# Twelve unit pairs a layer by seven quarter products, with their weight sums built in scratch memory by copies and accumulating transfers

## The chip, the core and the metric

The kernel runs on one core of one Trainium2 chip. The metric is the device time of one execution in microseconds; the median of the runs shown counts. The core has a matrix engine (PE in the profile, with its weight loads as PEld), a vector engine (DVE), a scalar engine (ACT), GpSimd (POOL) and SyncE (SP), which issues nearly all DMA transfers. Each engine works through its own list of instructions in order and waits at semaphores for the others.

## The reference

Two layers over 512 tokens of width 1024, all in float32. A layer has a mixing part (a gated DeltaNet of 8 heads, a windowed attention of 16 heads with a window of 128, a gated merge and an output projection) and a feed-forward part of width 4096:

```python
h2 = rmsnorm(x, pre_mlp_g)
ff = jnp.square(jax.nn.relu(h2 @ w_ff1)) @ w_ff2
return x + rmsnorm(ff, post_mlp_g)
```

The change concerns `h2 @ w_ff1`, a product of 512 x 1024 by 1024 x 4096, and what has to be ready for it.

## The kernel before

**Precision.** Every large product is made of three matmuls: each operand is split into a rounded high part and a rest, and high x high, high x rest and rest x high are added up in PSUM. A weight chunk (128 x 1024 elements, 512 KB) is loaded from the packed weights into a buffer `wr` (L282, six buffers), ACT makes the high part `wh` (L384), DVE the rest `wl` (L385), four buffers each. `prefetch` keeps four chunks ahead of their use.

**The stages of a layer.** First the input projections `ps_b`; then a mixing stage of 16 rounds (the loop `for i in range(16)`). Each round has one or two projections of the DeltaNet keys (`k_unit`) or the merge gates, and one of 16 attention groups (`att_group`: block `t` of 128 tokens, key head `g`, half `e`). For `t > 0` POOL masks the probabilities of the own block into `pc` (L1017) and PE uses them in `ps_o` (L1023). POOL also makes the rotary products (`rt`, L911 to L916) and the powers `irk` (L829). A head stage follows (8 DeltaNet heads, with small stores `fd` on POOL's queue), then the up projections and the output projection, and then the feed-forward part.

**The feed-forward part** runs over four slabs `s` of 1024 columns of `w_ff1`. Each slab is 8 units of 128 columns. A plain unit is 24 matmuls of 512 columns (8 blocks of rows, three matmuls each). A pair of units can instead be computed by seven products of quarters (a scheme of the Strassen kind): 7 x 4 x 3 = 84 matmuls of 256 columns, in `ff1`. For this the pair needs, beside its raw weights, the sums of quarters x0 to x3 (the two halves of the first unit and of the second): x0+x2, x0+x2+x3, x2+x3 and x0+x1+x2+x3, in two chunks `a` and `b`. Before, DVE makes them in SBUF from the two loaded chunks (L343, four additions of 128 x 512 a pair). `SEQ` says which units are paired: none in slab 0, two pairs in slab 1, three in slab 2 and four in slab 3, nine a layer. After slabs 0 to 2 the product with `w_ff2` follows, again by seven products (`mm_c`, P1 to P7), whose last half may be held back (`pending`) into the first pair of the next slab.

**What sets the order.** The kernel is written as one straight list of instructions over both layers. A scheduler then places them engine by engine by their dependences and its own model of times. An instruction that depends on nothing may be placed far ahead of where it is written; only blocks of the class `Order` (such as all matmuls in `ff1`) hold their written order. Transfers of SP's queue use eight completion counters in turn, those of POOL's queue eight others; a transfer waits for the one eight before it on its queue.

Of the kernel before, what the change touches and what calls it, by code (L numbers as in the profile page):

```python
# [15 lines left out]
ALU = mybir.AluOpType  # L16
# [25 lines left out]
WR = 6  # L42
FF_ORDER = (0, 4, 1, 5, 2, 6, 3, 7)
XB = 6
SEQ = (FF_ORDER, (0, 1, (4, 5), (2, 3), 6, 7), ((0, 1), (4, 5), (2, 3), 6, 7), ((0, 1), (2, 3), (4, 5), (6, 7)))

MIX = "G K K G K K G K K G K K G GA GA GA".split()
NA = sum(c.count("A") for c in MIX)
# [79 lines left out]
def hybrid_trunk(ctx, tc, x, positions, pre_mix_g, dn_conv_w, dn_a_log, dn_dt_bias, dn_norm_g,  # L128
# [44 lines left out]
    def PZ(name):  # L173
        return pp.tile([P, 512], F32, name=name, tag="ss", bufs=2)
# [147 lines left out]
    def up_specs(l, s):  # L322


        out = []

        def unit(m):
            return load(("w_ff1", l, 0, (s * 8 + m) * P, 0))

        def one(ms):  # L330
            b = {}

            def raw():
                b["0"], b["1"] = (unit(m) for m in ms)
                return b["0"]

            def of(n_):
                b[n_] = wp.tile([P, 1024], F32, name="wr", bufs=WR)
                x0, x1, x2, x3 = b["0"][:, :512], b["0"][:, 512:], b["1"][:, :512], b["1"][:, 512:]
                yb = b["a"][:, 512:]  # L340
                for o_, i0, i1 in (((b[n_][:, :512], x0, x2), (yb, b[n_][:, :512], x3)) if n_ == "a" else
                                   ((b[n_][:, 512:], x2, x3), (b[n_][:, :512], yb, x1))):
                    tt(out=o_, in0=i0, in1=i1, op=ALU.add)  # L343
                return b[n_]

            return raw, lambda: of("a"), lambda: of("b"), lambda: b["1"][:, 512:]

        last = None
        for n, e in enumerate(SEQ[s]):
            two = isinstance(e, tuple)  # L350
            if two:
                raw, fa, fb, tail = one(e)
            out.append((raw if two else lambda m=e: unit(m), 0))
            if last:
                out.append((last, -1))
            last = None
            if two:
                out += [(fa, 0), (fb, 0)]
                last = tail
        return out + [(last, -1)] * bool(last)  # L360

    specs = []
    for kind_, *key in chunk_order(depth):
# [241 lines left out]
    for l in range(depth):  # L605
# [435 lines left out]


        late, klate = (), []
        for i in range(16):
            us = []
            for c in MIX[i]:
                u = kind[c](n_[c])
                n_[c] += 1
                if u:
                    next(u)  # L1050
                    us.append(u)
            for u in klate:
                fin(u)
            klate = us
            g = att_group(*groups[i])
            next(g)
            fin(late)
            late = g
            if i > LASTK:
                steps(3)  # L1060
# [251 lines left out]
        for h in range(2):  # L1312
            d_keys(h)
            d_decay(h)
            d_turn(h)
        for h in range(H):
            if h < H - 2:
                d_keys(h + 2)
            d_inverse(h)
            d_load(h + 4)  # L1320
            d_chain(h)
            d_step(h - 2, h - 1)
            if h < H - 2:
                d_decay(h + 2)
                d_turn(h + 2)
            if h < H - 1:
                d_dense(h + 1)
# [12 lines left out]
            first.append((ps, mm_a(ps, yT, range(6))))  # L1340
        mT = []
        for m in range(KT):
            if m % 4 == 0:
                mq = UQ("mbr")
                sq = UQ("sgr") if m < NA2 else None
            qs = slice(m % 4 * 512, (m % 4 + 1) * 512)
            mb = mq[:, qs]
            dma(mb, mbd[m])
            if m < NA2:
                sga[m] = sq[:, qs]  # L1350
                dma(sga[m], gad[m])
            if m < 4:
                ps = first[m][0]
                mm_a(ps, yT, range(6, KT), first[m][1])
            else:
                ps = PM("ps_ud")
                mm_a(ps, yT)
            stt(out=sga[m], in0=sga[m], scalar=1.0, in1=ps, op0=ALU.add, op1=ALU.mult)
            tt(out=mb, in0=mb, in1=sga[m], op=ALU.add)
            p_ = pair(T[m % 4], "mT")  # L1360
            act(out=p_[0], in_=mb, func=AF.Copy, scale=0.5)
            stt(out=p_[1], in0=mb, scalar=0.5, in1=p_[0].bitcast(F32), op0=ALU.mult,
                op1=ALU.subtract)
            mT.append(p_)
# [100 lines left out]
        def ff1(done, rest=None):  # L1465


            order = Order(nc.tensor)
            order.begin()
            for n, e in enumerate(SEQ[s]):  # L1470
                if not isinstance(e, tuple):
                    ps = PM("ps_f1")
                    w = weights()
                    if rest is None and not any(isinstance(x, tuple) for x in SEQ[s][n + 1:n + 2]):
                        mm_a(ps, h2, w=w)
                        done((e,), ps)
                        continue
                    mm_a(ps, h2, range(4), w)
                    last = rest

                    def rest(ps=ps, w=w, e=e):
                        mm_a(ps, h2, range(4, 8), w)
                        done((e,), ps)

                    if last:
                        last()
                        rest()
                        rest = None
                    continue

                R = X4("raw")
                a, y, z, q = PM("ps_a"), PZ("ps_y"), PS("ps_z"), PK("ps_q")
                a, y, z, q = (b[:, half(0)] for b in (a, y, z, q))
                q_ = R[:, half(2)]
                c1 = weights()
                mm_h(a, c1, 0, ops["a11"], True)
                nc.scalar.copy(y, a)
                rest()

                def seventh():  # L1500
                    c = weights()
                    mm_h(q, c, 4, ops["n3"], True)
                    nc.scalar.copy(q_, q)
                    return c

                c2 = weights()
                mm_h(y, c2, 4, ops["n2"], False)
                nc.scalar.copy(z, y)
                mm_h(a, c1, 4, ops["a12"], False)
                act(out=R[:, half(0)], in_=a, func=AF.Relu)  # L1510
                if n > 0:
                    c3 = seventh()
                mm_h(z, c2, 0, ops["n1"], False)
                if n == 0:
                    c3 = seventh()
                act(out=R[:, half(3)], in_=z, func=AF.Copy, scale=-1.0)
                tt(out=R[:, half(3)], in0=R[:, half(3)], in1=q_, op=ALU.subtract)

                def rest(e=e, R=R, y=y, z=z, q_=q_, c3=c3):
                    mm_h(y, c3, 0, ops["a22"], False)  # L1520
                    tt(out=R[:, half(2)], in0=y, in1=q_, op=ALU.add)
                    act(out=R[:, 512:], in_=R[:, 512:], func=AF.Relu)
                    mm_h(z, weights(), 0, ops["n4"], False)
                    act(out=R[:, half(1)], in_=z, func=AF.Relu, scale=-1.0)
                    act(out=R, in_=R, func=AF.Square)
                    done(e, R)
            if rest:
                rest()
            order.end()

        cg = combos()
        for s in range(3):
# [9 lines left out]
            def lefts(X, Y):  # L1542

                a11, a21, a12, a22 = X[:, 0:512], X[:, 512:1024], Y[:, 0:512], Y[:, 512:1024]
                make("P1", T[5], a11)
                s1, s2 = T[4]("S1"), T[4]("S2")
                tt(out=s1, in0=a21, in1=a22, op=ALU.subtract)
                make("P5", T[7], s1)
                tt(out=s2, in0=a11, in1=s1, op=ALU.subtract)
                make("P6", T[1], s2)  # L1550
                make("P4", T[2], a22, -1.0)
                tt(out=s1, in0=a21, in1=a11, op=ALU.subtract)
                tt(out=s2, in0=a12, in1=s2, op=ALU.subtract)
                for name, src in (("P2", a12), ("P7", s1), ("P3", s2)):
                    later[name].append(src)
# [7 lines left out]
            def done(ms, ps):  # L1563
                if len(ms) == 2:
                    raw[ms[0] // 4] = ps
                else:
# [4 lines left out]
                    act(out=r_, in_=ps.rearrange("p (a n) -> p a n", a=2), func=AF.Relu)  # L1571
                    act(out=r_, in_=r_, func=AF.Square)
                count[0] += len(ms)
                if count[0] % 4 == 0:
                    lefts(*raw)

            if all(not isinstance(e, tuple) for e in SEQ[s]):
                for i, m in enumerate(SEQ[s]):
# [4 lines left out]
                        mm_a(ps, h2)  # L1583
                    done((m,), ps)
                    if s == 0 and i in (1, 3, 5):
                        next(cg)
            else:
                ff1(done, pending)
            pa = [PZ("ps_pa") for t in range(2)]
            mm_c(pa, left["P1"])  # L1590
            py = [PM("ps_py") for t in range(2)]
            for t in range(2):
                act(out=py[t], in_=pa[t], func=AF.Copy, scale=-1.0)
            make_later("P2", T[5])
# [99 lines left out]
```

## Time and profile before

| What | us |
|---|---|
| median of 3 runs | 1817.67 |
| lowest and highest of them | 1816.85 and 1820.55 |
| the profiled execution, its own time | 1816.19 |
| span of that execution, first to last instruction | 1814.5 |
| PE busy (and share of the span) | 1794.6 (99%) |
| DVE busy | 1375.1 (76%) |
| ACT busy | 1007.5 (56%) |
| POOL busy | 210.6 (12%) |
| DMA engines, share of the span for SP's queue | 49.2% |

Times in the profile count from the first instruction of the span. The mixing stage of layer 0 with its 16 rounds lies between about 45 and 240 us, the head stage up to 480, the feed-forward part of layer 0 from about 590 to 900; the second layer has the same stages some 900 us later. A row of a timeline has start and duration in us, the engine, the line, the operation, the tile written and the tiles read, and in brackets how long the engine had been idle before it and what ended that. A group's row has busy time and mean ns of one, then the idle time before and its releasers. In the list of waits stand the waiting instruction, what it waited for, the us in total, the times and the longest.

### The profile page before, as it was taken

How to read it: one execution, taken by the hardware profiler on the slowest of the kernel's cores; microseconds unless marked ns; L12 is line 12 of the kernel's file. 1: busy time of each engine (PE TensorE's matmuls, PEld its weight loads, DVE VectorE, ACT ScalarE, POOL GpSimd, SP SyncE). 2: the span in 40 equal slices, each digit the busy share in tenths (PEclk: the TensorE clock that was granted, in tenths of full speed). 3: DMA queues.
4: the chain of work that ended last, by engine and by line, in shares of the span. 5: the costliest groups of instructions: out<-in, count | busy, mean ns of one | idle time of the engine just before them, and what ended most of it. 6: DMA issues, size and time to landing. Idle time of an engine off the chain costs nothing.

```text
span 1814.5 us, 28394 instructions
## 1 busy us (share of the span) xinstructions
PE 1794.6 (99%) x10252; PEld 1524.7 (84%) x10252; DVE 1375.1 (76%) x2590; ACT 1007.5 (56%) x2065; POOL 210.6 (12%) x386
## 2 busy tenths in 40 slices
PE   9999999999999999999999999999999999999998
PEld 8878878888788888989898887888877888889896
DVE  5499796887666878898556997968875669698973
ACT  6678742444434656566556877234443347566572
POOL 0322102221101000000013221022111010000000
PEclk9999999999999999999999999999999999999999
DMA  5633447655463254554445334585545533555551
GB/s 201 203 112 121 111 146 226 178 172 152 117 208 129 82 164 156 174 180 145 168 160 176 106 127 111 169 232 159 163 140 154 171 116 105 174 162 164 174 178 56
DMA packets 146431, 278.60 MB, mean 154 GB/s; under 512 B 33569, under 2 KB 66657, under 8 KB 146290
## 3 DMA queue, kind: packets, MB, share of 16 engines
q1 hardware_dynamic: 145778, 276.75, 49.2%
q8 instruction: 81, 1.33, 0.3%
q14 instruction: 60, 0.49, 0.1%
q0 software_dynamic: 512, 0.03, 0.0%
HBM read 239.38 MB, written 37.36 MB: 153 GB/s over the span
## 4 chain that ended last, share of the span: by engine, by line
PE 88%; DVE 4%; ACT 4%; DMA 2%; issue 1%; POOL 0%; SPq 0%; DVEq 0%; POOLq 0%; ACTq 0%
PE ps_b L459 3%; PE ps_b L461 3%; PE ps_b L463 3%; PE ps_f L400 2%; PE ps_f L401 2%; PE ps_f L402 2%; PE ps_us L400 2%; PE ps_ud L400 2%; PE ps_us L401 2%; PE ps_ud L401 2%; PE ps_ud L402 2%; PE ps_us L402 2%; PE ps_vp L400 2%; PE ps_vp L402 2%; PE ps_vp L401 1%; PE ps_qp L401 1%
## 5 line engine op out<-in xcount | busy, mean ns | idle before, releaser
L384 ACT CAST wh<-wr 128x1024 fp32r<-128x1024 f32 (+2 forms) x368 | 372.7, 1019 | 430.4 <-PE ps_us L401 60.2
L385 DVE TENSOR_TENSOR wl<-wr,wh 128x1024 fp32r<-128x1024 f32 (+2 forms) x368 | 434.9, 1189 | 183.8 <-ACT wh L384 180.2
L526 POOL TENSOR_TENSOR pr<-pq,pw 128x1 f32<-128x1 f32 x16 | 9.8, 615 | 790.1 <-DVE pq L525 790.1
L459 PE MATMUL ps_b<-wh,h_h 128*128 128x432 f32 (+1 forms) x192 | 71.1, 370 | 0.0
L461 PE MATMUL ps_b<-wl,h_h 128*128 128x432 f32 (+1 forms) x192 | 70.4, 367 | 0.0
L463 PE MATMUL ps_b<-wh,h_l 128*128 128x432 f32 (+1 forms) x192 | 70.3, 366 | 0.0
L400 PE MATMUL ps_f<-g_h,wh 128*128 128x512 f32 x160 | 62.4, 390 | 0.0
L401 PE MATMUL ps_f<-g_l,wh 128*128 128x512 f32 x160 | 62.4, 390 | 0.0
L402 PE MATMUL ps_f<-g_h,wl 128*128 128x512 f32 x160 | 62.2, 389 | 0.0
L401 PE MATMUL ps_qp<-h_l,wh 128*128 128x512 f32 x128 | 53.9, 421 | 0.0
L400 PE MATMUL ps_vp<-h_h,wh 128*128 128x512 f32 x128 | 53.7, 420 | 0.0
L402 PE MATMUL ps_vp<-h_h,wl 128*128 128x512 f32 x128 | 53.7, 419 | 0.0
L995 ACT ACTIVATE M<-M,nm 128x128 f32<-128x128 f32 x128 | 49.8, 391 | 5.9 <-DVE nm L990 5.8
L400 PE MATMUL ps_qp<-h_h,wh 128*128 128x512 f32 x128 | 51.8, 405 | 0.0
L343 DVE TENSOR_TENSOR wr<-wr 128x512 f32<-128x512 f32 x72 | 47.5, 685 | 5.5 <-DMA wr<-in_weights_dram 5.2
L400 PE MATMUL ps_kp<-h_h,wh 128*128 128x512 f32 x128 | 51.6, 403 | 0.0
L402 PE MATMUL ps_qp<-h_h,wl 128*128 128x512 f32 x128 | 51.4, 401 | 0.0
L401 PE MATMUL ps_vp<-h_l,wh 128*128 128x512 f32 x128 | 51.3, 401 | 0.0
L401 PE MATMUL ps_ga<-h_l,wh 128*128 128x512 f32 x128 | 51.0, 398 | 0.0
L400 PE MATMUL ps_gb<-h_h,wh 128*128 128x512 f32 x128 | 51.0, 398 | 0.0
L402 PE MATMUL ps_kp<-h_h,wl 128*128 128x512 f32 x128 | 50.9, 398 | 0.0
L402 PE MATMUL ps_ga<-h_h,wl 128*128 128x512 f32 x128 | 50.7, 396 | 0.0
(435 smaller groups left out, 5928.4 us busy)
## 6 DMA issues: line engine op xcount, KB each, us to landing
wr<-in_weights_dram SPq DMA_DIRECT2D x320, 512.0 KB, 3.6
wr<-in_weights_dram SPq DMA_DIRECT2D x24, 432.0 KB, 5.2
D<-dd SPq DMA_DIRECT2D x32, 256.0 KB, 2.7
xd<-xo SPq DMA_DIRECT2D x12, 512.0 KB, 3.0
xt<-xd SPq DMA_DIRECT2D x24, 256.0 KB, 4.5
D<-gd SPq DMA_DIRECT2D x16, 256.0 KB, 6.2
dd<-D SPq DMA_DIRECT2D x16, 256.0 KB, 5.2
kkd<-kk SPq DMA_DIRECT2D x16, 256.0 KB, 2.0
```

Of the source, the lines that this page charges most:

```text
L343: tt(out=o_, in0=i0, in1=i1, op=ALU.add)
L384: nc.scalar.copy(wh[:, :w], wr[:, :w])
L385: sub(out=wl[:, :w], in0=wr[:, :w], in1=wh[:, :w].bitcast(F32), op=ALU.subtract)
L400: mm(ps, lhsT=wh[:, k, :], rhs=hi, start=k == 0, stop=False)
L401: mm(ps, lhsT=wh[:, k, :], rhs=lo, start=False, stop=False)
L402: mm(ps, lhsT=wl[:, k, :], rhs=hi, start=False, stop=k == KT - 1)
L459: mm(pss[t], lhsT=hi[:, tsl], rhs=wh[:, r, :], start=k == 0 and not onto, stop=False, skip_group_check=onto)
L461: mm(pss[t], lhsT=hi[:, tsl], rhs=wl[:, r, :], start=False, stop=False, skip_group_check=onto)
L463: mm(pss[t], lhsT=lo[:, tsl], rhs=wh[:, r, :], start=False, stop=k == KT - 1, skip_group_check=onto)
L526: ptt(out=r, in0=q1, in1=mhalf[:, 0:1], op=ALU.pow)
L995: act(out=M[:, j * P:(j + 1) * P], in_=M[:, j * P:(j + 1) * P], func=AF.Exp, bias=nm[:, j:j + 1], accum_out=den[:, j:j + 1])
```

## The change

All units of slabs 1, 2 and 3 are paired: 12 pairs a layer. The two chunks of sums are no longer made on DVE. For each of the 24 pairs there is a scratch tensor of 128 x 2048 in device memory (`fs` and a number: fs_112 to fs_123 are layer 0's pairs, fs_124 to fs_135 layer 1's in the built program), filled in four steps: two copies of the raw weights (L372, 512 KB each, SP's queue); an accumulating transfer from the weights (L374, 512 KB, POOL's queue); and two accumulating transfers inside the scratch tensor (L376 and L378, 256 KB each, POOL's queue). Each step reads what the step before has written. A generator `prepare(l)` issues them; it is advanced at 16 places of the layer: five in the mixing rounds, four among the heads, four among the up projections, three in slab 0. A pair then loads one raw chunk, the two chunks of sums and the second half of its other raw chunk. The halves of the sums have changed places, so the two products that use them swap their half. Beside this, the P1 operands are made as soon as their half of a slab is there, and two pairs of PSUM buffers change places for slabs 1 and 2.

```diff
-SEQ = (FF_ORDER, (0, 1, (4, 5), (2, 3), 6, 7), ((0, 1), (4, 5), (2, 3), 6, 7), ((0, 1), (2, 3), (4, 5), (6, 7)))
+FF_PAIRS = ((0, 1), (4, 5), (2, 3), (6, 7))
+SEQ = (FF_ORDER, FF_PAIRS, FF_PAIRS, ((0, 1), (2, 3), (4, 5), (6, 7)))
...
         def one(ms):
-            b = {}
-
-            def raw():
-                b["0"], b["1"] = (unit(m) for m in ms)
-                return b["0"]
-
-            def of(n_):
-                b[n_] = wp.tile([P, 1024], F32, name="wr", bufs=WR)
-                x0, x1, x2, x3 = b["0"][:, :512], b["0"][:, 512:], b["1"][:, :512], b["1"][:, 512:]
-                yb = b["a"][:, 512:]
-                for o_, i0, i1 in (((b[n_][:, :512], x0, x2), (yb, b[n_][:, :512], x3)) if n_ == "a" else
-                                   ((b[n_][:, 512:], x2, x3), (b[n_][:, :512], yb, x1))):
-                    tt(out=o_, in0=i0, in1=i1, op=ALU.add)
-                return b[n_]
-
-            return raw, lambda: of("a"), lambda: of("b"), lambda: b["1"][:, 512:]
+            d = sums[l, s, ms]
+
+            def of(c, w=1024):
+                wr = wp.tile([P, 1024], F32, name="wr", bufs=WR)
+                dma(wr[:, :w], d[:, c * 1024:c * 1024 + w])
+                return wr
+
+            def tail():
+                wr = wp.tile([P, 1024], F32, name="wr", bufs=WR)
+                dma(wr[:, :512], wpk[index["w_ff1", l, 0, (s * 8 + ms[1]) * P, 0], :, 512:])
+                return wr
+
+            return lambda: unit(ms[0]), lambda: of(0), lambda: of(1), tail
...
+    pairs = [(s_, e) for s_, seq in enumerate(SEQ) for e in seq if isinstance(e, tuple)]
+    sums = {(l, *p): dr.tile([P, 2048], F32, name=f"fs{l}{p[0]}{p[1][0]}")
+            for l in range(depth) for p in pairs}
+
+    def prepare(l):
+        def stages(s_, e):
+            i = index["w_ff1", l, 0, (s_ * 8 + e[0]) * P, 0]
+            assert index["w_ff1", l, 0, (s_ * 8 + e[1]) * P, 0] == i + 1
+            v = sums[l, s_, e][:, :].rearrange("p (h t c) -> p h t c", h=2, t=2)
+            for t in range(2):
+                dma(v[:, :, t, :], wpk[i + t].rearrange("p (h c) -> p h c", h=2))
+            yield
+            pdma(v[:, :, 1, :], wpk[i:i + 2, :, 0:512].rearrange("t p c -> p t c"), accum_op=ALU.add)
+            yield
+            pdma(v[:, 0, 0, :], v[:, 1, 1, :], accum_op=ALU.add)
+            yield
+            pdma(v[:, 1, 0, :], v[:, 0, 0, :], accum_op=ALU.add)
+
+        todo = [stages(*p) for p in pairs]
+        for n in range(len(todo) + 3):
+            for g in todo[max(n - 3, 0):n + 1]:
+                next(g, None)
+            yield
...
+        ready = prepare(l)
         for i in range(16):
+            if i % 3 == 1:
+                next(ready)
...
         for h in range(H):
+            if h % 2:
+                next(ready)
...
         for m in range(KT):
+            if m in (1, 3, 5, 7):
+                next(ready)
...
                 c2 = weights()
-                mm_h(y, c2, 4, ops["n2"], False)
+                mm_h(y, c2, 0, ops["n2"], False)
...
-                mm_h(z, c2, 0, ops["n1"], False)
+                mm_h(z, c2, 4, ops["n1"], False)
...
             def lefts(X, Y):
-                make("P1", T[5], a11)
...
                 count[0] += len(ms)
+                if ms[-1] in (1, 3):
+                    make("P1", T[5], raw[0][:, 0:512])
...
                     if s == 0 and i in (1, 3, 5):
+                        next(ready, None)
                         next(cg)
...
-            pa = [PZ("ps_pa") for t in range(2)]
+            pa = [(PM if s else PZ)("ps_pa") for t in range(2)]
...
-            py = [PM("ps_py") for t in range(2)]
+            py = [(PZ if s else PM)("ps_py") for t in range(2)]
```

Where the scheduler puts the new transfers, at three places of layer 0's mixing stage. (Lines of the changed file stand lower: L283 is the weight load L282, and 24 lines lower stand L802, that was L778, L1041 (L1017), L853 (L829) and L837 (L813).)

SP's list, around the first stores of keys `kkd`. Before:

```order
L282 DMA wr<-in_weights_dram 128x1024 x7
L813 DMA kkd<-kk 128x512
L816 DMA D<-dd 128x512
L282 DMA wr<-in_weights_dram 128x1024
L813 DMA kkd<-kk 128x512
```

Now:

```order
L283 DMA wr<-in_weights_dram 128x1024
L372 DMA fs_118<-in_weights_dram 256x512 x2
L283 DMA wr<-in_weights_dram 128x1024
L372 DMA fs_119<-in_weights_dram 256x512 x2
L372 DMA fs_120<-in_weights_dram 256x512 x2
L283 DMA wr<-in_weights_dram 128x1024
L372 DMA fs_121<-in_weights_dram 256x512 x2
L837 DMA kkd<-kk 128x512
```

Two to four copies stand between one weight load and the next. The copies begin behind the tenth weight load with fs_112 and end with fs_135, layer 1's last pair, all in this stage.

POOL's list a little later, with the counters that each instruction waits for (DMAHW: transfers of SP's queue, DMASW: those of POOL's):

```order
L374 DMA fs_121<-in_weights_dram 256x1x512 [waits DMAHW2_49,DMASW2_49]
L378 DMA fs_120<-fs_120 128x512 [waits DMASW0_49]
L853 TENSOR_TENSOR irk<-ssk,pw 128x4 [waits DVE_49]
L376 DMA fs_121<-fs_121 128x512 [waits DMAHW1_49,DMASW2_49]
L374 DMA fs_122<-in_weights_dram 256x1x512 [waits DMAHW7_49,DMASW5_49]
L378 DMA fs_121<-fs_121 128x512 [waits DMASW4_49]
L376 DMA fs_122<-fs_122 128x512 [waits DMAHW4_49,DMASW5_49]
```

Before, between two `irk` there stands no transfer. Now the three steps of a pair wait for one another on POOL, with one or two steps of a neighbouring pair between them.

POOL's list around the masks `pc` of rounds 8 and 9. Before:

```order
L829 TENSOR_TENSOR irk<-ssk,pw 128x4
L1017 AFFINE_SELECT pc<-pf_h 128x512
L1017 AFFINE_SELECT pc<-pf_l 128x512
L1017 AFFINE_SELECT pc<-pf_h 128x512
L1017 AFFINE_SELECT pc<-pf_l 128x512
```

Now:

```order
L1041 AFFINE_SELECT pc<-pf_h 128x512
L374 DMA fs_135<-in_weights_dram 256x1x512
L1041 AFFINE_SELECT pc<-pf_l 128x512
L378 DMA fs_134<-fs_134 128x512
L1041 AFFINE_SELECT pc<-pf_h 128x512
```

These are the two halves of the fifth mask and the first half of the sixth. The L376 of fs_135 stands behind them, between the two halves of the sixth, its L378 behind the sixth, and then, behind one `irk`, comes the seventh mask. Ahead of the first mask stand 47 of the 72 accumulating transfers, ahead of the seventh all of them.

## The prediction

> **What bounds the kernel now.** I read the page first, then the idle time of TensorE by place, then the DMA load by stretch.
>
> ```profile
> span 1814.5 us, 28394 instructions
> PE 1794.6 (99%) x10252; PEld 1524.7 (84%) x10252; DVE 1375.1 (76%) x2590; ACT 1007.5 (56%) x2065; POOL 210.6 (12%) x386
> PEclk9999999999999999999999999999999999999999
> DMA  5633447655463254554445334585545533555551
> q1 hardware_dynamic: 145778, 276.75, 49.2%
> q0 software_dynamic: 512, 0.03, 0.0%
> ```
>
> TensorE is busy for 99% of the span at full granted clock; no other engine comes near it. So only two things can move the end: fewer or shorter matmuls, or a wait that TensorE does not have now. Whether shorter matmuls pay must be read from starts, since a record of 0.39 us overlaps the next one. The timeline of TensorE, around one plain unit and one pair of the third slab of layer 0:
>
> ```profile
> 664.15 0.39 PE L400 MATMUL ps_f<-g_h,wh 128*128 128x512 f32 x1
> ...
> 672.31 0.28 PE L487 MATMUL ps_a<-g_h,wh 128*128 128x256 f32 x1
> ...
> 676.49 0.28 PE L487 MATMUL ps_y<-n_h,wh 128*128 128x256 f32 x1
> ...
> 692.33 0.40 PE L400 MATMUL ps_f<-g_h,wh 128*128 128x512 f32 x1
> ```
>
> From 664.15 to 672.31 stand 36 matmuls of 512 columns: 8.16 / 36 = 0.2267 us each. From 676.49 to 692.33 stand 132 of 256 columns: 15.84 / 132 = 0.1200 us each. Half the columns cost 53% of the time, not 50%.
>
> The stretches, with all engines' busy time, granted clock, share of the DMA engines and GB/s:
>
> ```profile
> core 0: us, PE busy (x) PEld busy (x) DVE busy (x) ACT busy (x) POOL busy (x), PEclk, DMA share, GB/s
> 17.00:128.00 111.00, 109.08 (x576) 97.07 (x575) 72.96 (x199) 76.81 (x201) 23.11 (x50) 1.00 0.49 162
> 128.00:185.00 57.00, 56.99 (x301) 46.44 (x299) 53.18 (x156) 45.46 (x136) 16.52 (x28) 1.00 0.40 121
> 600.00:900.00 300.00, 300.00 (x1698) 264.35 (x1697) 245.08 (x304) 186.98 (x293) 1.62 (x3) 1.00 0.48 157
> 17.00:22.00 5.00, 5.00 (x31) 4.81 (x30) 3.43 (x12) 2.99 (x9) 0.82 (x2) 1.00 0.96 342
> ```
>
> In the feed-forward stretch (600 to 900) TensorE is busy for all 300 us. The last row is the fastest DMA stretch I found: 342 GB/s at a share of 0.96, so 342 / 0.96 = 356 GB/s is the most that the 16 engines are seen to do.
>
> **The change, part by part.**
>
> *Three more pairs a layer, six in all.* Two plain units are 48 matmuls of 512 columns, 48 x 0.2267 = 10.88 us; a pair is 84 of 256, 84 x 0.1200 = 10.08 us. Gain 0.80 us a pair, 6 x 0.80 = 4.8 us, all of it on the path, since TensorE has no idle time there.
>
> *The sums on VectorE go away.*
>
> ```profile
> L343 DVE TENSOR_TENSOR wr<-wr 128x512 f32<-128x512 f32 x72 | 47.5, 685 | 5.5 <-DMA wr<-in_weights_dram 5.2
> ```
>
> 47.5 us of VectorE leave, and 6 x 1.5 splits of a whole chunk come in. Both lie beside the matmuls of the feed-forward stretch, where VectorE has 55 of 300 us free; worth nothing either way. The swapped halves of the sums, the earlier P1 and the exchanged PSUM buffers are reorderings inside that same full stretch: nothing. If that cover were gone, the 5.2 us of waits in this row are what could return.
>
> *The weights of a pair.* Before, a pair loads 2 x 512 KB; now 3 x 512 + 256 KB, 1.84 MB in 10.08 us, 182 GB/s. That is half of 356, so it hides under the matmuls.
>
> *The building of the sums.* This decides. A pair has two copies of 512 KB from weights to scratch on SP's queue and three accumulating transfers of 512, 256 and 256 KB on POOL's: 2 x 0.524 = 1.05 MB copied and 1.05 MB added. For 24 pairs that is 25.2 MB copied and 25.2 MB added. The text of the kernel spreads them over each layer, but as the rows of the built order show (the section on the change), the scheduler puts the transfers of both layers, all 24 pairs, into the first layer's mixing stage. They begin behind the first weight loads at about 17 us, and the last accumulate stands on POOL ahead of the seventh pair of L1017 (L1041 in the new file), the masked copies of attention scores. In the trace these are:
>
> ```profile
> 127.81 0.64 POOL L1017 TENSOR_SCALAR_AFFINE_SELECT pc<-pf_h 128x512 fp32r<-128x512 f32 x1 [0.76 <-ACT pf_h L500]
> ...
> 185.17 0.63 POOL L1017 TENSOR_SCALAR_AFFINE_SELECT pc<-pf_h 128x512 fp32r<-128x512 f32 x1 [3.22 <-ACT pf_h L500]
> ```
>
> The first of them is at 127.8 us and the seventh at 185.2 us. Their readers are matmuls; by line, and in the list of waits:
>
> ```profile
> L1023 PE MATMUL ps_o<-pc,vp x24: 387/397/504, 131.0 to 236.8; 128*128 128x512 f32 x24
> PE ps_o L1023 <- POOL pc L1017: 0.6, 1, 0.6
> PEld ps_o L1023 <- POOL pc L1017: 4.7, 14, 1.0
> ```
>
> TensorE already waits for them now and then, by up to 1.0 us: there is no reserve. POOL works in order, and each accumulate waits there until the one before it of its pair has landed. So 72 accumulates must be through by 185.2 us; whatever they are late is late for TensorE. Behind the waiting POOL stand the rotary products, the 1/norms and the masks; behind a late weight load on SP stand the splits and every matmul.
>
> The room for them, by the DMA view of 17 to 185 us:
>
> ```profile
> DMA packets 12639, 24.83 MB, mean 148 GB/s; under 512 B 1680, under 2 KB 4816, under 8 KB 12624
> q1 hardware_dynamic: 12624, 24.65, 45.4%
> q8 instruction: 7, 0.11, 0.3%
> q14 instruction: 8, 0.07, 0.1%
> wr<-in_weights_dram SPq DMA_DIRECT2D x23, 512.0 KB, 4.0
> ```
>
> The engines now use 45.8% of the 168 us, 77 us; 91 us are free. No row shows a copy from device memory to device memory, nor an accumulate. Bounds by the nearest rows: at the least each byte costs one pass at the best rate, 25.2 / 0.356 = 71 us for the copies and 71 for the accumulates: 77 + 71 + 71 = 219, 51 us too many. At the most a copy is two passes (it reads and writes the same memory) and an accumulate three (it reads two operands and writes one): 77 + 141 + 212 = 430, 262 too many. I take one pass for a copy, as for a load, and two for an accumulate, because it fetches two operands for each result: 77 + 71 + 141 = 289, 121 us too many.
>
> The Trainium skill, in "Collectives: The Full Stack", The bandwidth ceiling: the fold count and why AG ≠ RS ≠ AR, says that a sum inside a DMA costs not the addition but the second read, which halves the rate; by it the accumulates cost the 141 us that I take, where the row of a load would give 71. Its page "DMA: Bandwidth & Descriptors", Latency and other measured facts, gives 207 to 214 GB/s for copies between HBM tensors; by 214 the copies are 118 us and the sum 168 too many. No run here shows either yet.
>
> *Other costs of the 120 new transfers.* The nearest row for one on POOL's queue is the 2 KB store of the head's scale:
>
> ```profile
> L1216 POOL DMA_DIRECT2D fd<-ff x16: 590/620/757, 348.9 to 1393.3; - x16
> DMA to landing us min/median/max: 1.7/2.4/4.5
> ```
>
> 0.62 us of issue, x72 = 45 us of POOL, beside the 23 + 17 us that it is busy in the two windows: 85 of 168, not the bound. The second layer's mixing stage gets no transfers, so it stays as it is.
>
> **Sum.** The profiled execution has 1816.2 us, 1.7 more than its span; - 4.8 + 121 = 1932.4. It lies 1.5 under the median of 1817.7, so against the median I predict 1934, slower.
>
> **Rivals.**
>
> *All hidden (the other side).* The transfers find gaps, nothing reaches TensorE and only the matmuls count: 1817.7 - 4.8 = 1812.9. For it: the engines are free for 91 of the 168 us, and behind 240 us nothing is added but 0.79 MB a pair. Against it: 50.3 MB in the free 91 us would be 553 GB/s, over the 356 seen. It decides at the first L1041: if POOL has issued its 47 earlier accumulates by 127.8 us, this is right. Partly hidden, with up to 8 us left over, it reads as no change.
>
> *The chain, not the bytes.* The transfers are cheap, and only the order on POOL counts. A step takes the 2.4 us of the small store to land, plus its bytes at 356 GB/s: (2.4 + 1.47), (2.4 + 0.74), (2.4 + 0.74), 10.2 us a pair. With two pairs under way that is 24 x 10.2 / 2 = 122 us, against 168 less the 40 that POOL is busy, 128: not late at all. With 1.25 under way, about what the built order allows near its end (a step waits for the one before, and one step of the next pair fits between), 195 - 128 = 67 us late. For it: each wait on POOL is of this kind. Against it: it needs the DMA engines to have room, which the sum denies. Its middle, 4 to 47 us late, gives 1817 to 1860; below that it is the case before.
>
> *Heavy transfers.* Two passes for a copy and three for an accumulate: 1817.7 - 4.8 + 262 = 2075. For it: every byte is read from and written to the same memory. Against it: loads and stores of this trace go at one pass each.
>
> *It does not do what it says.* The pairs are built once and read later, so the spread in the text would be the truth only if the scheduler kept it; the built order shows that it does not, so this has no chance of its own.
>
> **How the numbers follow.** Forecast, +50 to +210 us, 64%; chain or light transfers, 1817 to 1860, 13%; heavy, over 2030, 12%; all hidden 6%; partly hidden 5%. The predicted time is 1934. The range takes in the light end and most of what lies above: 1826 to 2040. A change of 0.2%, 3.6 us, is about what a measurement can tell from none. Faster by more: 0.06; within: 0.06, the partly hidden and a piece of the light case; slower: 0.88.
>
> **What would show it.** In the profile after: DMA tenths of 8 and 9 in the first 5 to 8 slices, and TensorE's busy tenths under 9 there; `ps_o` waiting for `pc` for tens of us in total, with the POOL row before it released by a DMA; the q0 row with 25 MB or more; the stretch of feed-forward of both layers shorter by 2.4 us each and full. The second layer's mixing stage as long as before, 240 us. I am wrong if the seventh `pc` stands before 200 us, or if the feed-forward stretch, and not the first 250 us, holds the loss.

## The result and the profile after

The changed kernel takes 2000.0 us (median of 4 runs, 1998.6 to 2005.9), the kernel before 1818.0 us: 1.1005 times as long, 95% interval 1.098 to 1.103. I had predicted 1934 us in a range from 1826 to 2040. The direction and the place were right; the loss is 182 us where I had said 116.

The page of the changed kernel, the rows that answer to those quoted of before:

```profile
span 2004.2 us, 29122 instructions
PE 1816.7 (91%) x10468; PEld 1548.6 (77%) x10468; DVE 1347.5 (67%) x2542; ACT 1024.4 (51%) x2101; POOL 275.6 (14%) x458
PE   9475045899999999999999999999999999999998
PEclk9787567899999999999999999999999999999999
DMA  9899789547655553456574543447554543556672
q0 software_dynamic: 13952, 25.20, 8.8%
```

TensorE was busy for 99% of the span and is now for 91%. Nearly all of its gaps lie in the first eight slices of 50 us; the DMA engines are at 7 to 9 tenths in seven of them, and behind them both rows look as before. The accumulating transfers are the 25.2 MB of q0.

Two stretches by engine, with the columns of the prediction's stretches: from the first weight loads to the issue of the last accumulate, and the 112 us behind it.

```profile
17.00:368.00 351.00, 182.63 (x835) 155.12 (x835) 120.38 (x334) 117.19 (x319) 100.53 (x148) 0.75 0.94 211
368.00:480.00 112.00, 111.16 (x516) 89.76 (x515) 89.90 (x247) 60.69 (x166) 14.76 (x20) 1.00 0.50 140
```

For 351 us the DMA engines are 94% used and TensorE works for 183 us. Right behind the issue of the last accumulate TensorE is full again, 111.2 of 112 us. What it waited for in those 351 us, and POOL ahead of its transfers (us in total, times, longest):

```profile
PE ps_o L1047 <- POOL pc L1041: 108.4, 9, 66.9
POOL fs L376 <- DMA fs<-in_weights_dram: 113.9, 20, 11.1
POOL fs L378 <- DMA fs<-fs: 93.9, 22, 8.1
```

The masks `pc` are most of what TensorE waits for, 108 of the 168 us that it is idle there, and POOL, which makes them, waits for landings. Other work stands behind the accumulates too. TensorE waited 25.5 us once for a split `wh` on ACT and 33 us at three steps of the attention; ACT itself waited, in the same stretch, 59 us for POOL's rotary products and 30 us for POOL's `D` (L802). POOL's timeline at the first mask and around the last accumulate, and the group of the matmuls that read the masks:

```profile
265.53 0.93 POOL L1041 TENSOR_SCALAR_AFFINE_SELECT pc<-pf_h 128x512 fp32r<-128x512 f32 x1
...
367.49 0.83 POOL L378 DMA_DIRECT2D fs<-fs  x1 [3.33 <-DMA fs<-fs]
...
374.36 0.64 POOL L1041 TENSOR_SCALAR_AFFINE_SELECT pc<-pf_h 128x512 fp32r<-128x512 f32 x1 [2.42 <-ACT pf_h L524]
```

```profile
L1047 PE MATMUL ps_o<-pc,vp x24: 389/496/797, 266.5 to 429.0; 128*128 128x512 f32 x24
```

The first mask stood at 127.8 us and now stands at 265.5, with 47 accumulates ahead of it. The seventh stood at 185.2 us and now stands at 374.4, behind the last accumulate. The last `ps_o` of the layer moves from 236.8 to 429.0: 192 us late. From there on next to nothing more is lost. The feed-forward stretch, from its first to its last `ps_f`, of layer 0 before and after:

```profile
578.85 0.28 PE L411 MATMUL ps_f<-g_h,wh 128*128 128x256 f32 x1
...
909.49 0.39 PE L424 MATMUL ps_f<-wh,h_l 128*128 128x512 f32 x1
```

```profile
770.36 0.28 PE L435 MATMUL ps_f<-g_h,wh 128*128 128x256 f32 x1
...
1099.71 0.39 PE L448 MATMUL ps_f<-wh,h_l 128*128 128x512 f32 x1
```

330.64 us become 329.35, 1.3 less; layer 1's likewise. The profiled executions differ by 2004.2 - 1814.5 = 189.7 us: 192 lost in the mixing stage of layer 0, 2.6 won by the matmuls.

### The profile page after: what moved, and what is told of

Read it like the earlier page. It is cut to its first block, busy times and chain, and to the rows that moved or that the text cites. A ratio compares the mean times of both kernels' runs of the same rounds, so it can differ in the third digit from the quotient of the medians.

```text
span 2004.2 us, 29122 instructions
## 1 busy us (share of the span) xinstructions
PE 1816.7 (91%) x10468; PEld 1548.6 (77%) x10468; DVE 1347.5 (67%) x2542; ACT 1024.4 (51%) x2101; POOL 275.6 (14%) x458
## 4 chain that ended last, share of the span: by engine, by line
PE 71%; DMA 13%; DVE 6%; issue 5%; ACT 3%; POOL 2%; SPq 0%; DVEq 0%; POOLq 0%; ACTq 0%
DMA fs<-in_weights_dram 7%; DMA fs<-fs 3%; PE ps_b L483 2%; PE ps_b L485 2%; PE ps_b L487 2%; PE ps_us L424 1%; PE ps_vp L424 1%; PE ps_vp L426 1%; PE ps_us L425 1%; PE ps_us L426 1%; PE ps_vp L425 1%; PE ps_ud L425 1%; PE ps_ud L426 1%; PE ps_ud L424 1%; PE ps_qp L424 1%
## 5 line engine op out<-in xcount | busy, mean ns | idle before, releaser
L1047 PE MATMUL ps_o<-pc,vp 128*128 128x512 f32 x48 | 21.5, 484 | 109.6 <-POOL pc L1041 109.6
L483 PE MATMUL ps_b<-wh,h_h 128*128 128x432 f32 (+1 forms) x192 | 72.3, 377 | 25.5 <-ACT wh L408 25.5
L483 PEld LDWEIGHTS ps_b<-wh,h_h 128*128 128x128 f32 x192 | 36.8, 192 | 29.2 <-ACT wh L408 25.8
L511 PE MATMUL ps_z<-n_h,wh 128*128 128x256 f32 x192 | 54.9, 286 | 0.0
L514 PE MATMUL ps_a<-g_h,wl 128*128 128x256 f32 x192 | 54.3, 283 | 0.0
L513 PE MATMUL ps_a<-g_l,wh 128*128 128x256 f32 x192 | 54.3, 283 | 0.0
L514 PE MATMUL ps_z<-n_h,wl 128*128 128x256 f32 x192 | 54.3, 283 | 0.0
L513 PE MATMUL ps_z<-n_l,wh 128*128 128x256 f32 x192 | 54.3, 283 | 0.0
L511 PE MATMUL ps_a<-g_h,wh 128*128 128x256 f32 x192 | 54.3, 283 | 0.0
L425 PE MATMUL ps_kp<-h_l,wh 128*128 128x512 f32 x128 | 53.9, 421 | 0.0
L975 DVE SCALAR_TENSOR_TENSOR qT<-ps_q,qT 64x512 fp32r<-64x512 f32 x32 | 22.0, 688 | 47.0 <-ACT qT L974 46.3
```

The costliest lines, as they stand in the source:

```text
L425: mm(ps, lhsT=wh[:, k, :], rhs=lo, start=False, stop=False)
L483: mm(pss[t], lhsT=hi[:, tsl], rhs=wh[:, r, :], start=k == 0 and not onto, stop=False, skip_group_check=onto)
L511: mm(ps, lhsT=wh[:, k0 + k, :], rhs=hi, start=start and k == 0, stop=False, skip_group_check=True)
L513: mm(ps, lhsT=wh[:, k0 + k, :], rhs=lo, start=False, stop=False, skip_group_check=True)
L514: mm(ps, lhsT=wl[:, k0 + k, :], rhs=hi, start=False, stop=k == 3, skip_group_check=True)
L1047: mm(po, lhsT=v_[:, o_ + g * P:o_ + (g + 1) * P], rhs=a, start=i == 0, stop=i == len(pvs) - 1)
```

## The experiments

The theory on record: both layers' transfers stand in one stage, and their bytes are too many for the DMA engines there. The rivals: the waits of POOL from step to step and not the bytes; transfers that cost wherever they stand. Of e2, e3, e7 and e8 there is one execution each; those of one kernel otherwise lie within 0.6% of one another.

### e1: every transfer in its written place

```diff
-                dma(v[:, :, t, :], wpk[i + t]...)
+                tc.keep_in_program_order(dma(v[:, :, t, :], wpk[i + t]...))
-            pdma(v[:, :, 1, :], ..., accum_op=ALU.add)
+            tc.keep_in_program_order(pdma(v[:, :, 1, :], ..., accum_op=ALU.add))
...
```

> Each of the 120 new transfers is kept behind the instruction that the program writes ahead of it on its queue; nothing else is changed, so each layer's 12 pairs are built within that layer, one step of a pair per place. If the loss comes from putting both layers' transfers into the first mixing stage, the DMA engines have room (about 78 us of copies and 174 us of accumulates, worked out from the packets of the changed kernel, in two layers of 580 us that are about half used) and only the shorter matmuls are left: 1813 us, 1810 to 1820. If these transfers cost wherever they stand (POOL waits for a landing, the engines collide with loads), 25 to 50 us of the loss of 182 come back in each layer: 1860 to 1920.

1885.2 us, 1.0365 times the kernel before (1.0347 to 1.0382). 115 of the 182 us come back, so the first stage was the place of most of the loss; but 69 stay, which the theory did not allow. The time lies in the range of the second expectation, transfers that cost wherever they stand. Three stretches:

```profile
120.00:180.00 60.00, 59.64 (x321) 49.14 (x321) 55.66 (x160) 47.67 (x139) 21.37 (x33) 1.00 0.68 177
360.00:480.00 120.00, 106.29 (x655) 87.58 (x656) 80.28 (x160) 42.63 (x82) 28.47 (x34) 0.90 0.60 171
600.00:900.00 300.00, 299.31 (x1883) 271.07 (x1882) 239.83 (x297) 196.23 (x316) 8.14 (x11) 1.00 0.57 185
```

The mixing and the feed-forward stages are full. The head stage is not, with the DMA engines only 60% used. The loss there is the subject of e5 and e6.

### e2: the same transfers without the addition

```diff
-            pdma(v[:, 0, 0, :], v[:, 1, 1, :], accum_op=ALU.add)
+            pdma(v[:, 0, 0, :], v[:, 1, 1, :])
...
```

> The three accumulating transfers of a pair are plain copies of the same bytes, with the same queue, order and waits; the sums are left out, so the output isn't the reference's. If the bytes bound the changed kernel, an accumulated packet of 2 KB (226 ns in the mean there) becomes one of about 104 ns, 174 us of the 16 engines become 80: 77 + 78 + 80 = 235 against the 168 us there are, 67 too many, up to 20 more for idle ends: 1880 to 1900 us. If the chain of 72 waits on POOL decides and not the bytes, nothing but the landing of a step gets a little shorter: 1950 to 2000.

1929.2 us, between the two. The DMA view and the stretch from 17 us to the issue of the last transfer:

```profile
q0 software_dynamic: 7216, 24.91, 33.3%
```

```profile
17.00:290.00 273.00, 175.06 (x831) 149.28 (x830) 118.91 (x331) 116.31 (x317) 77.70 (x147) 0.81 0.89 271
```

And the same rows of the changed kernel, from 17 to 368 us:

```profile
q0 software_dynamic: 13296, 24.91, 49.3%
q1 hardware_dynamic: 25407, 49.05, 44.4%
```

The same 24.9 MB take 33.3% of 273 = 91 us as plain copies and 49.3% of 351 = 173 us as accumulates: 1.9 times. (The last 256 KB of the 25.2 MB move behind these windows.) The addition is not the only difference: the plain transfers went in about half as many packets, 7216 against 13296, so in packets about twice as large. How the factor divides between the two was not tried apart.

71 us of the loss come back. By the bytes alone 94 were to come back. Of the accumulates' engine time 82 us went; but with lighter transfers the engines are used for 89% of the time only, 30 us idle where the changed kernel has 21. So the waits have a share too. The next run measures it.

### e7: the same bytes, with the steps of a pair far apart on POOL

```diff
-        for n in range(len(todo) + 3):
-            for g in todo[max(n - 3, 0):n + 1]:
-                next(g, None)
+        for n in range(len(todo) + 7):
+            for m, g in enumerate(todo):
+                if n - m in (0, 1, 4, 7):
+                    next(g, None)
...
+            tc.add_manual_dep(i.ins, steps_[-1].name, ...)
```

> Both layers' transfers in the first mixing stage as in the changed kernel, the same bytes, but on POOL a step stands eight transfers behind the one it needs (two in the changed kernel). If the bytes bound it, 330 us of engine time from 17 us on end at 347 at the earliest against 368 in the changed kernel, so 20 us come back at most: 1975 to 2000 us. If the waits of POOL bound it (208 us of idle time ahead of the steps), most of them go, the masks come early: 1860 to 1930.

1955.6 us, outside both ranges: 44 come back, twice what the full engines were to allow, and 138 stay.

```profile
17.00:323.00 306.00, 180.05 (x879) 153.56 (x878) 127.98 (x367) 124.35 (x344) 103.26 (x149) 0.80 1.02 247
```

```profile
q0 software_dynamic: 13250, 24.83, 51.0%
```

```profile
321.89 0.81 POOL L386 DMA_DIRECT2D fs<-fs  x1 [3.30 <-DMA fs<-fs]
...
323.46 0.92 POOL L1050 TENSOR_SCALAR_AFFINE_SELECT pc<-pf_h 128x512 fp32r<-128x512 f32 x1
```

What POOL waited for at the two later steps of a pair, which was 208 us in the changed kernel:

```profile
  POOL fs L386: 26.0, 8
  POOL fs L384: 3.7, 2
```

Now the engines have no idle time on average (a share of 1.02), POOL's waits from step to step are down from 208 to 30 us, and the seventh mask still stands directly behind the last accumulate, at 323.5 us in place of 374.4. So 138 of the 182 stay when the engines are full and most of this waiting is gone; I put these down to the bytes. The other 44 came back with the order on POOL. 38 of them can be seen: 21 us of idle engines (6% of 351) in the changed kernel, and accumulates that took 173 us of engine time there and 51.0% of 306 = 156 here. Why the same bytes are cheaper here, no run tells.

### e3: the copies alone

```diff
-            pdma(v[:, :, 1, :], ..., accum_op=ALU.add)
+            pass
...
```

> The three accumulating transfers are left out, the copies stay where the scheduler put them; the sums are missing, so the output isn't the reference's. By the bytes: 77 + 78 = 155 us against 168, so nothing is late for long: 1813 us, up to 1825. If the copies between the weight loads of SP's queue make the loads late by themselves (24 loads that land in 11 us in place of 4), 1850 to 1900.

1814.7 us (the kernel before beside it 1816.5). The stretch where copies and loads are thickest:

```profile
60.00:120.00 60.00, 57.63 (x299) 48.34 (x298) 45.66 (x115) 44.13 (x124) 18.02 (x39) 1.00 1.01 342
```

With full DMA engines TensorE goes on at its former pace, 57.6 us of 60 where the kernel before had 58.1 in the same stretch. Here full engines for 60 us cost nothing that can be measured. The copies that the scheduler put between the weight loads are free by themselves; it takes the accumulates on top of them to make the loss.

### e8: only layer 0's pairs by transfers

```diff
+            if l:
+                return raw, lambda: add(0), lambda: add(1), lambda: b[3][:, 512:]
...
-        ready = prepare(l)
+        ready = iter(range(16)) if l else prepare(l)
```

> Layer 0's 12 pairs by transfers, in the first mixing stage where the scheduler puts them; layer 1's sums on DVE. By the bytes there is a threshold: 77 + 39 + 87 = 203 us against 168, 35 too many, 10 for idle ends, 2.8 for DVE's sums in layer 1, less 1.3: 1865 us, 1850 to 1875. If each accumulate costs the same share, half of the 187: 1911 us, 1895 to 1925.

1901.6 us: not the 1865 of the bytes, and inside the range of the second expectation, 1895 to 1925. So this run does not favour the bytes over an equal share for each accumulate. It does refute the point in time that I had worked with. On POOL:

```profile
205.10 0.81 POOL L396 DMA_DIRECT2D fs<-fs  x1 [4.88 <-DMA fs<-fs]
...
210.22 0.85 POOL L1059 TENSOR_SCALAR_AFFINE_SELECT pc<-pf_h 128x512 fp32r<-128x512 f32 x1
```

```profile
17.00:206.00 189.00, 118.49 (x591) 104.16 (x590) 75.85 (x216) 78.82 (x209) 49.02 (x72) 0.82 0.94 232
```

Here all 36 accumulates stand ahead of the first mask, which was due at 127.8 us and not, like the seventh, at 185.2. It comes at 210.2, 82 us late, and the run is 84 us longer than before. 94% of 189 = 178 us of engine time lie ahead of it, in a room of 111. With this room the terms of the expectation give nearly what was measured, 49% of 111 = 54 for other transfers, 39 and 87, 10 for idle ends: 79 us too many. But that was worked out after the result.

### e4: the pairs alone, sums on DVE

```diff
-            d = sums[l, s, ms]
...
+                for o_, i0, i1 in (((hi, x0, x2), (lo, hi, x3)) if c == 0 else
+                                   ((hi, x2, x3), (lo, b[0][:, :512], x1))):
+                    tt(out=o_, in0=i0, in1=i1, op=ALU.add)
...
-        ready = prepare(l)
+        ready = iter(range(16))
```

> All 24 pairs, but their sums made on DVE as before, with no copies, no scratch and no accumulating transfers. Measures the matmul term alone: 6 pairs by 0.80 us, 4.8 us faster: 1813 us. Rival: the 24 more sums of 0.69 us and two raw chunks per pair make the splits late in slabs 1 and 2, 0 to 5 us given back: 1813 to 1819.

1822.0 us, 1.0027 times the kernel before (1.0017 to 1.0038): slower by 0.3%, outside of both expectations. The sums now take 63.1 us of DVE in place of 47.5. The third slab shows

```profile
720.00:810.00 90.00, 88.57 (x544) 78.86 (x543) 83.38 (x106) 57.22 (x88) 0.00 (x0) 1.00 0.52 165
```

DVE is busy for 83 of 90 us there, and TensorE has gaps that add up to 1.4 us; the whole feed-forward stretch takes 333.3 us (from 581.0 to 914.3) against 330.6. I read this as DVE being late in the slabs of pairs; it was not tried apart. More pairs without the transfers don't pay: the sums are needed off DVE.

### e5: in place, and the 1/norm ahead of the inverse's copies on POOL

In e1 the scheduler had also exchanged two steps on POOL in the head stage. POOL's timeline of one head in e3, which has the order of before, and in e1:

```profile
348.20 1.29 POOL L1242 TENSOR_TENSOR ff<-ff,pw 128x4 f32<-128x4 f32 x1 [3.64 <-DMA ff<-sd]
349.80 0.76 POOL L1243 DMA_DIRECT2D fd<-ff  x1 [0.30 <-POOL ff L1242]
351.32 0.68 POOL L1164 COPY T<-Tc 32x128 f32<-32x128 f32 x2 [0.76 <-PE ps_i L1125]
```

```profile
438.80 1.59 POOL L1164 COPY T<-Tc 32x128 f32<-32x128 f32 x2 [24.39 <-PE ps_i L1125]
440.47 1.36 POOL L1242 TENSOR_TENSOR ff<-ff,pw 128x4 f32<-128x4 f32 x1
442.13 0.65 POOL L1243 DMA_DIRECT2D fd<-ff  x1 [0.30 <-DMA kxd<-kvx]
```

The 1/norm `ff` waits for a matmul that it has nothing to do with. The edit on top of e1:

```diff
-            pdma(fd[h, :]..., ff)
+            dn["fd", h] = pdma(fd[h, :]..., ff).ins
...
-                    nc.gpsimd.tensor_copy(T6v[r, :, r], Tcv[r, ah, :])
+                    c_ = nc.gpsimd.tensor_copy(T6v[r, :, r], Tcv[r, ah, :]).ins
+                    if ("fd", h - 2) in dn:
+                        tc.add_manual_dep(c_, dn["fd", h - 2].name, ...)
```

> As e1 (each transfer in its written place), and the copies L1164 of the inverse are kept behind the 2 KB store L1243 of the head two before, the order on POOL that the kernel before has and e1 lost. If e1's loss in the head stage (62 us in two layers) comes from that exchange, which made the 1/norm wait for a matmul and its round trip through memory end the chain, a head takes 23.3 us again in place of 28 to 29: 1885 - 62 = 1823 us, 1815 to 1832. If it comes from the transfers themselves (big packets ahead of the small round trips, POOL waiting for landings), 1860 to 1885.

1870.8 us, 1.0292 times the kernel before (1.0277 to 1.0308): by the medians the exchange is worth about 14 of e1's 69 us (e1's runs spread over 11), and the time lies in the range of the second expectation, the transfers themselves. In the chain of work that ended last the small round trip through memory now stands, a 2 KB store `fd` and a read `fb` behind it. One head of e5, in which a pair's transfers are issued, and SP's list shortly ahead of its store:

```profile
374.36 1.04 POOL ff L1245
...
375.69 4.58 DMA fd<-ff
380.29 6.91 DMA fb<-fd
```

```profile
371.87 0.50 SPq L372 DMA_DIRECT2D fs<-in_weights_dram  x1
...
373.81 0.50 SPq L372 DMA_DIRECT2D fs<-in_weights_dram  x1
```

The stretch of the read, in the columns of the stretches:

```profile
380.30:387.20 6.90, 2.97 (x16) 2.17 (x15) 1.55 (x6) 1.99 (x4) 1.64 (x2) 0.91 0.95 159
```

The store takes 4.6 us and the read 6.9, 11.5 together. Two copies of 512 KB were issued just ahead of the store, the three accumulates 3.4 us behind it (rows below), and during the read the DMA engines were 95% busy. The next head, without transfers, needed 3.9 + 3.3 = 7.2 us for the same. One store alone says little: over all 16 heads its median went from 2.4 us (at most 4.5) in the kernel before to 3.9 in e5. What DVE (`yf`) waited for `fb` in all heads, before and in e5, says more:

```profile
  DVE yf L1220: 23.4, 10
```

```profile
  DVE yf L1250: 70.6, 16
```

47 us more, against a loss of 53. Copies and accumulates come together here; which of them delays the round trip was not tried apart. `qe`, once a head, shows the step:

```profile
354.42 1.27 POOL L1223 TENSOR_TENSOR qe<-qq,egb 128x512 f32<-128x512 f32 x1
...
377.88 1.28 POOL L1223 TENSOR_TENSOR qe<-qq,egb 128x512 f32<-128x512 f32 x1
379.11 0.88 POOL L378 DMA_DIRECT2D fs<-fs  x1
...
408.25 1.27 POOL L1223 TENSOR_TENSOR qe<-qq,egb 128x512 f32<-128x512 f32 x1
```

23.5 us for a head without transfers, 30.4 for the next, which starts with them. The other two heads of this layer that can be measured so, with transfers, took 24.9 and 29.7, the other two without 24.9 and 23.8; in the kernel before a head takes 22.6 to 23.3. So not every group of transfers delays a head alike. 18 of the 53 us are lost behind the heads, between the first up projection and the feed-forward part; there too a read `fb`, of 8.8 us, stands in the chain.

### e6: in place, but not among the heads

```diff
-            if i % 3 == 1:
+            if i % 2 == 1:
                 next(ready)
...
-            if h % 2:
-                next(ready)
...
-            if m in (1, 3, 5, 7):
-                next(ready)
...
+                if (s, *ms) in ((1, 0, 1), (1, 2, 3), (2, 0, 1), (2, 2, 3), (2, 6, 7)):
+                    next(ready)
-                    if s == 0 and i in (1, 3, 5):
-                        next(ready, None)
+                    if s == 0 and i in (1, 5):
+                        next(ready)
```

> In place, but at other places: eight in the mixing rounds, two in slab 0, two in slab 1 and three in slab 2, none among the heads and the up projections. If only the head and up stages of e1 were hurt (62 + 14 us), the transfers are hidden: 1814 us, 1812 to 1820, what e3 has without the sums. If the extra transfers cost wherever they stand, about half of e1's 70 us stay: 1840 to 1860.

1813.5 us, 0.9978 times the kernel before (0.9970 to 0.9987): 0.2% faster than the kernel before, little but clear of the noise, and 9% faster than the changed kernel.

```profile
span 1812.8 us, 29145 instructions
PE   9999999999999999999999999999999999999998
DMA  6769948655455777666546787485545566976661
```

The same bytes and the same additions as in the changed kernel, spread over both layers and away from the heads and the up projections, are hidden altogether. This shows that it was the places among the heads and the up projections that cost e1 and e5 their time. That the reason is the small round trip on which the next step waits is what e5's rows suggest; a run with the same places and a faster or protected round trip was not made.

## Why the prediction was right in kind and too small

**The place and the mechanism** are confirmed. Nearly all signs came as written: DMA tenths of 7 to 9 in seven of the first eight slices, TensorE's gaps in the same ones, 108 us of `ps_o` waiting for `pc`, 25.2 MB on q0, the seventh mask behind 200 us. Only the feed-forward stretch became 1.3 us shorter in place of 2.4. From layer 0's last `ps_f` to layer 1's first, nothing was lost worth naming: 568.6 us before, 569.5 after. e3 and e6 show that neither the copies nor the bytes as such cost anything; the accumulates ahead of the masks do. One run was not made: the same transfers in the same stage, with POOL's masks and rotary products ahead of them or on another engine. So that POOL's order carries the loss to TensorE is read from the rows, not from a run.

**The failed step is the sum's term for the accumulates, and the assumption of full engines behind it.** My sum was 77 + 71 + 141 = 289 us in a room of 168. Measured in the 351 us:

- Other transfers and copies: 44.4% of 351 = 156 us. Without the 76 of before (45.4% of 168), if those cost what they did before, 80 for the copies, where I had 71. I had taken one pass at the best rate that the trace of before shows, 356 GB/s; over the whole stage it is 25.2 MB in 80 us, 315 GB/s.
- Accumulates: 173 us, where I had 141. Two passes was about the right count: the same bytes without the addition take 91 us (e2), 1.9 times less, and the copies on SP's queue, as many bytes, 80, 2.2 times less. Again the pass was too cheap.
- Idle engines: 21 us, where I had none. With the steps further apart (e7) they are gone. So they are the chain on POOL, which I had named as a rival of its own and not as an addition to the bytes.

76 + 80 + 173 + 21 = 350: 182 us over the room. That the loss of the medians is 182 too is chance: this execution, the slowest of the four, lost 189.7. 7 us more go by from the last accumulate to the seventh mask, and 3 up to the last of the stage.

**The price of the addition.** The Trainium skill, "Collectives: The Full Stack", The bandwidth ceiling: the fold count and why AG ≠ RS ≠ AR, says of a collective's reduce step that the second read and not the addition is the price, and that it halves the rate. 173 against 91 us agrees with about half the rate; whether it is the read or the addition, no run here shows, as e2 leaves out both. The 207 to 214 GB/s of "DMA: Bandwidth & Descriptors", Latency and other measured facts, for copies between HBM tensors is not what this kernel had: 80 us for 25.2 MB, by the difference above, where that rate gives 118.

**The matmuls.** 4.8 us were to be won, 2.6 were. The pitch of the matmuls was not what failed, it is still 0.120 and 0.227 us in the changed kernel: a layer's 144 matmuls of 512 columns became 252 of 256, 2.4 us by it. The stretch became 1.3 us shorter; the missing 1.1 us a layer are small gaps that I could not put down to one wait.

**DVE's sums "worth nothing either way".** Wrong in one direction: e4 shows that 24 pairs with their sums on DVE are 5 us slower than the 18 of before; DVE's 55 free of 300 us are a mean, and the third slab had 7 of 90 left. Taking the sums off DVE is what makes the additional pairs pay, by 0.2%, where the transfers are hidden (e6).

**Issue on POOL.** I had 0.62 us a transfer, 45 in all, from a small store. The rows of the changed kernel:

```profile
L374 POOL DMA_DIRECT2D fs<-in_weights_dram x24: 1057/1342/1923, 30.3 to 352.9; - x24
L376 POOL DMA_DIRECT2D fs<-fs x24: 805/826/1147, 40.2 to 362.7; - x24
```

With 48 of the short kind and 24 of the long, 72 us. It was not the bound, as said.

**The rivals.** "Heavy transfers" (two passes for a copy, three for an accumulate) is out by the sizes, 80 and 173 us and not 141 and 212, though 173 lies about midway between my 141 and its 212; the factor of about two between accumulate and copy, and not one and a half, speaks against it. The total alone does not: 2000 lies about midway between 1934 and its 2075. "The chain, not the bytes" is out as the main cause and right as an addition: 44 of 182 us came back in e7. "All hidden" is what e6 has, 1813.5 against 1812.9 worked out, and that it fits so closely is partly luck: e6's two feed-forward stretches are 2.3 us shorter and not 4.8. Its condition, the transfers through ahead of the masks, did not hold in the changed kernel (first mask at 265.5 us). What I had not asked was whether the written order, had the scheduler kept it, would have been free: e1 says no, by 69 us.

## What to carry to other kernels

A transfer that depends on nothing but weights has no place of its own: a scheduler may issue all of them at the first chance, so look in the built order for which in-order queue they stand in and what stands behind them. Work out engine time up to the first instruction that is needed behind them, at the rate of a whole stage and not of its best stretch, and add the idle time of waits from step to step. And where such transfers are moved to, look for small round trips through memory on which the next step waits, not only for free bandwidth on average.

## What was not expected of the hardware

- Accumulates of the same 24.9 MB took 173 us of engine time when each stood close behind the one it needs (the changed kernel) and 156 when they were eight apart (e7); plain copies, in about half as many packets, 91 (e2). Spread over both layers the 25.2 MB took 8.8% of 1812.8 = 160 us (e6). What makes the difference of 17 is open.
- With copies and accumulates issued around it, a 2 KB store and the 256 KB read behind it took 11.5 us, in the next head, without them, 7.2 (e5). The DMA engines were only about 60% used over the head stage (e1's rows), but 95% in the 6.9 us of that read: free engine time on average did not protect it.
- With the DMA engines at a share of 1.01 and 342 GB/s, TensorE kept its pace (e3).
- The granted TensorE clock fell to 0.75 on average in the 351 us in which TensorE had gaps, and was 1.00 right behind them. It was not measured what that adds; TensorE was the one that waited.
